# A hybrid trunk on one core: the samples' new SSD state is written to the increment's tile and stored from there; low parts of fresh y blocks read the transposed block in PSUM

## The chip, the cores and the metric

One core of one Trainium2 chip runs the whole program, both layers, in one launch. The metric is the device time of an execution in microseconds (us). The kernel before was run three times; one further execution was profiled, and all rows below are of that one.

## What is computed

A trunk of two layers works on a prompt of 2048 tokens and on 8 samples of one token each, with the same weights. Cut to what matters here:

```python
def _layer(x, ...):
    u = _rmsnorm(x, norm_w) @ w_in                 # 1024 -> 4880, columns split among the groups
    ...
    ya = mLSTM group  (512 wide), times its gates
    yb = SSD group    (512 wide), times its gate, normed
    yc = sliding-window attention with sinks (512 wide), times its gate
    y = concat([ya, yb, yc]) @ w_out               # 1536 -> 1024
    return x + y, states

def _ssd step:  h_t = exp(dt_t A) h_{t-1} + dt_t x_t B_t^T ;  y_t = h_t C_t
```

The outputs are y of the prompt and of the samples and every state array after the step; for the samples that includes the new SSD state h of each layer and sample (8 heads x 64 x 128 values).

## The kernel before, in words

**Blocks and chunks.** The prompt goes through in blocks of 512 tokens, four to a layer, eight in all; below, "the first out phase" is the out projection of block 0 of layer 0, and so on to the eighth. Every large product is a sum of three fp32r products of high and low parts. The weights come in chunks of 128 rows: `load_chunk` brings a chunk, `split_chunk` makes its high part on ScalarE (line 494) and low part on GpSimd (line 498) the first time, and `multiply` does 12 matmuls of 128x512 into four PSUM banks (`pj`; line 519 where the weights stream, line 521 where they stand still). An out phase has 24 chunks, two halves of the output by the 12 blocks k of y (k = 0 to 3 mLSTM, 4 to 7 SSD, 8 to 11 attention). For all but the last block of the trunk, the out phase of a block comes after the first five column groups (g0, qk, v, o, z) of the next block; after it come x0, x1, cq, cz, bz.

**Side streams.** The mixing of a block (mLSTM `a`, SSD `b`, attention `c`), the convolution `v`, gates, norms and the samples' work `d` are Python generators. `pump` takes a step of one of them between matmuls when a planner's model of the engines (`Clock`: its costs for each engine, and when the next of the four other PSUM banks, `mx`, is free) says so; `drain` forces a stream to its end at a few chunks: `b` at the last chunk of v, `a` at that of o, `a` and `d` at that of cq, and `c` ahead of the first chunk of an out phase. A scheduler then orders every engine's instructions. So a change of one instruction's operands can move others.

**prep_y (line 1243).** Ahead of each out chunk it makes the high and the low part of a y block. The first time a block k < 8 is used (half 0: 64 such fresh blocks in the program), it lies token-major: TensorE transposes it into an `mx` bank `pt` (4 x line 1252), ScalarE writes the high part `yh` from the bank (line 1259), and ScalarE copies the bank back into the block (line 1263). For every block VectorE then makes the low part `yl` = block x norm weight - `yh` from SBUF (line 1266, `low`, put off by half a chunk). The chunk's matmuls need `yh` first and `yl` for the third product of each tile.

**dec_b (line 1477).** The SSD step of the 8 samples, in the second out phase of each layer. Each sample b has three tiles of a set, `h`, `t`, `bb`, and the two sets take turns. The steps are: SyncE loads the old state of sample b+1 into `h` (line 1547) and its broadcast B and C into `bb` (line 1548, from `bcd`); GpSimd `h` = h x exp(dt A) (1560); VectorE `t` = B x (dt x) (1562); GpSimd `h` = h + t (1564); SyncE stores `h` (1566); VectorE `t` = h x C (1567) and reduces `t` to y (1568). The load of sample b+2 into the same `h` therefore waits for the store of sample b to land.

**dec_c (line 1588)** is the samples' attention in the first out phase of each layer: scores are multiplied on GpSimd (1659), reduced on VectorE into `dST` (1661), and transposed on TensorE for the softmax (1667, 1668).

Of the kernel before, what the change touches and what calls it, by code (L numbers as in the profile page):

```python
# [16 lines left out]
ALU = mybir.AluOpType  # L17
AX = mybir.AxisListType
# [166 lines left out]
class Build:  # L185
# [1057 lines left out]
    def prep_y(self, ch):  # L1243

        nc, S, k = self.nc, ch['S'], ch['k']
        Y, L = [S['yA'], S['yB'], S['yC']][k // 4], S['L']
        blk = Y[:, :, (k % 4) * 128:(k % 4) * 128 + 128] if k < 8 else Y[:, k % 4, 0:512].rearrange("p (t c) -> p t c", c=128)
        new = ch['new']
        if new:
            pt = self.mx()  # L1250
            for t in range(4):
                nc.tensor.transpose(pt[:, t * 128:t * 128 + 128], blk[:, t, :], self.ident)  # L1252
            pt = pt.rearrange("p (t c) -> p t c", c=128)
        else:
            pt = blk
        i = k % 2

        yh, yl = (self.xTh[i], self.xTl[i]) if S['last'] else self.F[2 * i:2 * i + 2]
        nc.scalar.activation(yh.rearrange("p (t c) -> p t c", c=128), pt, AF.Copy, scale=L['ynw'][:, k:k + 1])  # L1259

        if new:

            nc.scalar.activation(blk, pt, AF.Copy)  # L1263

        def low():
            nc.vector.scalar_tensor_tensor(yl.rearrange("p (t c) -> p t c", c=128), blk, L['ynw'][:, k:k + 1],  # L1266
                                           yh.bitcast(F32).rearrange("p (t c) -> p t c", c=128),
                                           op0=ALU.mult, op1=ALU.subtract)

        self.late.append((0, low))  # L1270
        ch['y'] = (yh, yl)
# [205 lines left out]
    def dec_b(self, l, L, D):  # L1477
        nc, I, O, U = self.nc, self.I, self.O, self.U[5:]
        TT = nc.vector.tensor_tensor
# [18 lines left out]
        for half in range(2):  # L1498
# [9 lines left out]
            acc, t = xc[:, half * 4:half * 4 + 4, :], self.s([128, 4, 8], "dct")  # L1508
# [30 lines left out]
        yT = self.s([128, 8, 4], "dyT")  # L1539
        yield  # L1540

        def sets(b):
            return [U[(1 + 3 * (b % 2) + i) % 6][:, 0:512] for i in range(3)]

        def load(b):
            h, t, bb = sets(b)
            nc.sync.dma_start(h.rearrange("p (j s) -> p j s", s=128), I['state_ssm'][l, b].rearrange("(j h) p s -> (h p) j s", h=2))
            nc.sync.dma_start(bb, bcd[b].partition_broadcast(128))
# [3 lines left out]
        for b in range(8):  # L1552
            if b < 7:
                load(b + 1)
            h, t, bb = sets(b)
            h3, t3 = [x.rearrange("p (j s) -> p j s", s=128) for x in (h, t)]
            Bv, Cv = [bb[:, i * 256:i * 256 + 256].rearrange("p (g s) -> p g s", s=128).unsqueeze(2).to_broadcast([128, 2, 2, 128])
                      for i in range(2)]
            t4, h4 = [x.rearrange("p (g j s) -> p g j s", g=2, s=128) for x in (t, h)]
            nc.gpsimd.tensor_tensor(h3, h3, dAp[:, b, :].unsqueeze(2).to_broadcast([128, 4, 128]), op=ALU.mult)  # L1560
            xb = dtp[:, b, :].unsqueeze(2).to_broadcast([128, 4, 128]).rearrange("p (g j) s -> p g j s", g=2)
            TT(t4, Bv, xb, op=ALU.mult)
            yield
            nc.gpsimd.tensor_tensor(h, h, t, op=ALU.add)
            yield
            nc.sync.dma_start(O['s_h'][l, b].rearrange("(j h) p s -> (h p) j s", h=2), h3)
            TT(t4, h4, Cv, op=ALU.mult)
            nc.vector.tensor_reduce(yT[:, b, :], t3, AX.X, ALU.add)
            yield
        xD = self.s([128, 8, 4], "dxD")  # L1570
        TT(xD, xT.rearrange("p j b -> p b j"), Dp.unsqueeze(1).to_broadcast([128, 8, 4]), op=ALU.mult)
# [5 lines left out]
        t = U[0][:8, 0:512]  # L1577
# [358 lines left out]
```

## Time and profile before

| | us |
|---|---|
| three runs: median (lowest to highest) | 2995.44 (2991.24 to 2997.36) |
| the profiled execution: its own time | 2994.12 |
| its span in the profile | 2992.3 |
| TensorE busy within the span | 2903.5 (97%) |
| VectorE, ScalarE, GpSimd busy | 1912.3, 1235.0, 920.3 |

The span is what the profile covers; 1.8 us of the execution lie outside it. A row of a timeline gives start, duration, engine, line, operation and tiles, and in brackets the idle time of the engine just before it with what ended that. A row of a table of stretches gives the busy time of each engine within the stretch.

### The profile page before, as it was taken

To read this page: it belongs to the slowest core of one execution; us is meant where nothing else is said; L and a number is where in the kernel's file an instruction comes from. 1 tells how busy PE (TensorE), PEld (TensorE's weight loads), DVE (VectorE), ACT (ScalarE), POOL (GpSimd) and SP (SyncE) were. 2 spreads that over 40 slices of the span, in tenths; PEclk is the share of its full clock that TensorE was granted. 3 is DMA by queue.
4 is the path that set the end of the run, shared out by engine and by line. 5 is a ranking of instruction groups with operands and counts; after the bars stand their busy time and mean duration, and the time that the engine had idled before them with its cause. 6 is when DMAs were issued, how large, how long until landed. Compare 5 with 4: busy or idle time off the path is not lost.

```text
span 2992.3 us, 42253 instructions
## 1 busy us (share of the span) xinstructions
PE 2903.5 (97%) x14454; PEld 2373.4 (79%) x14454; DVE 1912.3 (64%) x4323; ACT 1235.0 (41%) x3219; POOL 920.3 (31%) x968
## 2 busy tenths in 40 slices
PE   8999999999999999999999999999999999999988
PEld 7787877788878888888788778887887778788876
DVE  6378567778476763477644686477755677645774
ACT  5343555235432453325544345432444225532344
POOL 5336325244131430116422552332421132200321
PEclk9999999999999999999999999999999999999999
DMA  8755558754575434655556745687545754355533
GB/s 279 241 197 168 174 184 284 248 170 141 164 247 189 151 117 143 199 171 182 184 187 215 240 159 183 205 274 232 161 156 177 244 174 160 131 163 165 177 112 124
DMA packets 245995, 558.82 MB, mean 187 GB/s; under 512 B 49308, under 2 KB 82236, under 8 KB 245732
## 3 DMA queue, kind: packets, MB, share of 16 engines
q1 hardware_dynamic: 245780, 556.12, 57.6%
q8 instruction: 114, 1.87, 0.3%
q14 instruction: 101, 0.83, 0.1%
HBM read 430.46 MB, written 127.87 MB: 187 GB/s over the span
## 4 chain that ended last, share of the span: by engine, by line
PE 71%; DVE 13%; DMA 8%; POOL 3%; ACT 2%; issue 2%; SPq 1%; POOLq 0%; DVEq 0%; ACTq 0%
PE pj L519 29%; PE pj L521 27%; DMA wr<-in_w_in 2%; PE mx L1203 2%; PE mx L1152 2%; PE mx L984 1%; DMA unit<-bcd 1%; DVE quad L659 1%; PE mx L542 1%; PE mx L541 1%; POOL hl L498 1%; ACT unit L1173 1%; PE mx L993 1%; PE mx L1252 1%; DMA unit<-us 1%
## 5 line engine op out<-in xcount | busy, mean ns | idle before, releaser
L521 PE MATMUL pj<-hl,xTh 128*128 128x512 f32 (+1 forms) x3072 | 945.4, 383 | 17.2 <-ACT hl L494 7.6
L519 PE MATMUL pj<-xTh,hl 128*128 128x512 f32 x2240 | 727.5, 402 | 4.8 <-ACT xTh L1259 2.9
L521 PEld LDWEIGHTS pj<-hl,xTh 128*128 128x128 f32 x3072 | 564.6, 189 | 129.0 <-DVE quad L562 8.3
L521 PE MATMUL pj<-hl,xTl 128*128 128x512 f32 (+1 forms) x1536 | 580.4, 381 | 0.0
L519 PE MATMUL pj<-parts,hl 128*128 128x512 f32 x2016 | 518.9, 404 | 15.1 <-DVE parts L1266 8.3
L519 PEld LDWEIGHTS pj<-xTh,hl 128*128 128x128 f32 x2240 | 421.5, 190 | 100.9 <-ACT xTh L1259 3.9
L519 PEld LDWEIGHTS pj<-parts,hl 128*128 128x128 f32 x2016 | 366.9, 189 | 96.1 <-DVE parts L1266 11.2
L519 PE MATMUL pj<-xTl,hl 128*128 128x512 f32 x1120 | 436.0, 398 | 1.9 <-DVE xTl L1266 1.9
L498 POOL TENSOR_TENSOR hl<-wr,hl 128x512 fp32r<-128x512 f32 (+1 forms) x232 | 318.9, 1380 | 356.3 <-ACT hl L494 311.2
L521 PEld LDWEIGHTS pj<-hl,xTl 128*128 128x128 f32 x1536 | 291.1, 189 | 52.5
L1195 POOL TENSOR_TENSOR parts<-parts,cst 128x512 fp32r<-128x512 f32 x120 | 158.6, 1339 | 409.0 <-ACT parts L1188 392.3
L519 PEld LDWEIGHTS pj<-xTl,hl 128*128 128x128 f32 x1120 | 211.2, 189 | 47.7 <-DVE xTl L1266 2.3
L1266 DVE SCALAR_TENSOR_TENSOR parts<-quad,lp,parts 128x512 fp32r<-128x512 f32 x168 | 143.0, 852 | 155.4 <-ACT quad L1263 62.4
L494 ACT ACTIVATE hl<-wr 128x512 fp32r<-128x512 f32 (+1 forms) x232 | 142.2, 615 | 234.2 <-PE mx L542 49.6
L1032 POOL TENSOR_TENSOR unit<-quad,rpqn 128x256 f32<-128x256 f32 x32 | 24.3, 759 | 441.6 <-PE mx L951 166.8
L1173 ACT ACTIVATE unit<-unit,c_m,c_sc 128x128 f32<-128x128 f32 x256 | 123.3, 483 | 69.3 <-DVE c_m L1164 68.8
L1259 ACT ACTIVATE parts<-quad,lp 128x512 fp32r<-128x512 f32 x112 | 80.4, 720 | 155.9 <-PE pj L519 141.1
L659 DVE SCALAR_TENSOR_TENSOR quad<-quad,lp,quad 128x512 f32<-128x512 f32 x192 | 141.8, 781 | 0.3
L1189 DVE TENSOR_TENSOR parts<-mx,parts 128x512 fp32r<-128x512 f32 x64 | 44.0, 687 | 90.2 <-ACT parts L1188 81.0
L384 POOL TENSOR_TENSOR quad<-quad 128x512 f32<-128x512 f32 x24 | 33.5, 1398 | 217.1 <-ACT quad L382 216.4
L1181 ACT ACTIVATE unit<-unit,c_m 128x128 f32<-128x128 f32 x256 | 81.3, 392 | 19.4 <-DVE c_m L1179 19.2
L541 PE MATMUL mx<-hl,samS 128*66 128x512 f32 (+1 forms) x208 | 83.4, 403 | 0.9 <-ACT hl L494 0.9
(409 smaller groups left out, 4551.3 us busy)
## 6 DMA issues: line engine op xcount, KB each, us to landing
hl<-kept SPq DMA_DIRECT2D x552, 512.0 KB
kept<-hl SPq DMA_DIRECT2D x184, 512.0 KB
wr<-in_w_in SPq DMA_DIRECT2D x168, 256.0 KB
hl<-kept SPq DMA_DIRECT2D x48, 272.0 KB
quad<-in_xT SPq DMA_DIRECT2D x40, 256.0 KB
quad<-in_x_prompt SPq DMA_DIRECT2D x16, 512.0 KB
wr<-in_w_out SPq DMA_DIRECT2D x32, 256.0 KB
x<-quad SPq DMA_DIRECT2D x32, 256.0 KB
```

The costliest lines, as they stand in the source:

```text
L494: nc.scalar.activation(h, r, AF.Copy)
L498: nc.gpsimd.tensor_tensor(lw, r, h.bitcast(F32), op=ALU.subtract)
L519: nc.tensor.matmul(ps[t], w[:, tt], a, start=st and first, stop=en and last)
L521: nc.tensor.matmul(ps[t][:, :N], a[:, tt], w[:, :N], start=st and first, stop=en and last)
L541: nc.tensor.matmul(pd[:66, :N], self.samS[:, k, :], hi[:, :N], start=st, stop=False)
L659: nc.vector.scalar_tensor_tensor(acc, u[:, j:j + 512], cw[:, j, c:c + 1], acc, op0=ALU.mult, op1=ALU.add)
L1152: nc.tensor.matmul(o, q, kz[:, a, s, 0:nk, :].rearrange("p n c -> p (n c)"), start=s == 0, stop=s == 1)
L1173: nc.scalar.activation(P(a, j), P(a, j), AF.Exp, bias=nm[:, j:j + 1], scale=head(sc, a, j), accum_out=den[:, j:j + 1])
L1181: nc.scalar.activation(P(a, j), P(a, j), AF.Copy, scale=den[:, j:j + 1])
L1195: nc.gpsimd.tensor_tensor(o.bitcast(F32R), p, self.triu.unsqueeze(1).to_broadcast([128, 4, 128]), op=ALU.mult)
L1259: nc.scalar.activation(yh.rearrange("p (t c) -> p t c", c=128), pt, AF.Copy, scale=L['ynw'][:, k:k + 1])
L1266: nc.vector.scalar_tensor_tensor(yl.rearrange("p (t c) -> p t c", c=128), blk, L['ynw'][:, k:k + 1], yh.bitcast(F32).rearrange("p (t c) -> ...
```

## The change

```diff
@@ prep_y
         def low():
-            nc.vector.scalar_tensor_tensor(yl.rearrange("p (t c) -> p t c", c=128), blk, L['ynw'][:, k:k + 1],
+            nc.vector.scalar_tensor_tensor(yl.rearrange("p (t c) -> p t c", c=128), pt, L['ynw'][:, k:k + 1],
                                            yh.bitcast(F32).rearrange("p (t c) -> p t c", c=128),
                                            op0=ALU.mult, op1=ALU.subtract)
@@ dec_b
-            nc.gpsimd.tensor_tensor(h, h, t, op=ALU.add)
-            yield
-            nc.sync.dma_start(O['s_h'][l, b].rearrange("(j h) p s -> (h p) j s", h=2), h3)
-            TT(t4, h4, Cv, op=ALU.mult)
-            nc.vector.tensor_reduce(yT[:, b, :], t3, AX.X, ALU.add)
+
+            nc.gpsimd.tensor_tensor(t, h, t, op=ALU.add)
+            yield
+            nc.sync.dma_start(O['s_h'][l, b].rearrange("(j h) p s -> (h p) j s", h=2), t3)
+            TT(h4, t4, Cv, op=ALU.mult)
+            nc.vector.tensor_reduce(yT[:, b, :], h3, AX.X, ALU.add)
             yield
```

In `prep_y` the low part of the 64 fresh blocks takes its first operand from the PSUM bank `pt` in place of the block in SBUF (for other blocks `pt` is the block, and nothing changes). In `dec_b` the new state is written over `t`, stored from `t`, and the product with C goes to `h`. From line 1564 on, a line of the changed kernel has a number one higher.

No engine gets an instruction more or less. The order of the instructions moves in two long stretches, from the start of each layer's first out phase to the end of its second (438 to 891 us of the profile, and 1917 to 2367 us; the tables of the profile cut them into eight, four to a layer: the first out phase, the chunks x0 to bz, g0 to z, the second out phase); elsewhere a few rows move. Three places:

**TensorE, start of the sixth out phase (layer 1, block 1).** `mx_21084` and `mx_21130` are the banks of the transposed y blocks k = 0 and 1, `hl_20995` the last chunk of bz, `hl_21032` the first out chunk, `mx_21000` and `mx_21051` banks of the attention's mixing. Before:

```order
L521 MATMUL pj_20938<-hl_20981,xTh_110 128x512
L1252 MATMUL mx_21084<-ident,quad_100 128x128
L1203 MATMUL mx_21051<-parts_94,vd 128x512
L1252 MATMUL mx_21084<-ident,quad_100 128x128 x3
L521 MATMUL pj_20935<-hl_20995,xTh_111 128x512
```

With the change:

```order
L1203 MATMUL mx_21000<-parts_93,vd 128x512
L521 MATMUL pj_20938<-hl_20995,xTh_111 128x512
L1203 MATMUL mx_21000<-parts_94,vd 128x512
L1203 MATMUL mx_21051<-parts_91,vs 128x512
L1252 MATMUL mx_21084<-ident,quad_100 128x128 x4
L1203 MATMUL mx_21051<-parts_92,vs 128x512
L1252 MATMUL mx_21130<-ident,quad_100 128x128 x4
L1203 MATMUL mx_21051<-parts_93,vd 128x512
L519 MATMUL pj_21124<-parts,hl_21032 128x512 x2
```

The transposes of k = 0 stood ahead of all 12 matmuls of the last bz chunk; now they stand behind it, and behind them only the four of k = 1 and two of the mixing come ahead of the out phase's first matmul.

**TensorE, the softmax transposes of dec_c, layer 0.** `hl_5452` is the last chunk of x1, `hl_5481` the first of cq, `hl_5635` the last of cq. Before:

```order
L519 MATMUL pj_5365<-xTh_111,hl_5452 128x512
L1667 MATMUL mx_5687<-ident,dST_5258 64x128
L1668 MATMUL mx_5687<-ident,unit_84 64x128
L521 MATMUL pj_5568<-hl_5481,xTh_104 128x512
```

With the change (the same two, one line number higher):

```order
L521 MATMUL pj_5561<-hl_5612,xTh_110 128x512
L1668 MATMUL mx_5712<-ident,dST_5378 64x128
L1669 MATMUL mx_5712<-ident,unit_84 64x128
L521 MATMUL pj_5558<-hl_5635,xTh_111 128x512
```

They moved from ahead of the first cq chunk to ahead of the last one, seven chunks or 84 matmuls later; in layer 1 they moved alike.

**VectorE, dec_b of layer 1 around samples 2 and 3.** `unit_85` to `unit_87` are h, t, bb of the even samples, `unit_88`, `unit_89`, `unit_84` those of the odd ones. Before:

```order
L792 TENSOR_TENSOR rtA_21443<-mx_21439,cst 120x512
L1562 TENSOR_TENSOR unit_86<-unit_87,ddt_21333 128x512
L1562 TENSOR_TENSOR unit_89<-unit_84,ddt_21333 128x512
L838 TENSOR_TENSOR unit_83<-mx_21446,X_20560 128x256
L1266 SCALAR_TENSOR_TENSOR parts_92<-quad_97,lp_2958,parts_91 128x512
L1567 TENSOR_TENSOR unit_86<-unit_85,unit_87 128x512
```

With the change:

```order
L1568 TENSOR_TENSOR unit_88<-unit_89,unit_84 128x512
L1266 SCALAR_TENSOR_TENSOR parts_92<-quad_97,lp_2958,parts_91 128x512
L838 TENSOR_TENSOR unit_83<-mx_21446,X_20560 128x256
L1569 TENSOR_REDUCE dyT_21342<-unit_88 128x4
L1562 TENSOR_TENSOR unit_86<-unit_87,ddt_21333 128x512
L1266 SCALAR_TENSOR_TENSOR parts<-quad_97,lp_2958,parts 128x512
L1562 TENSOR_TENSOR unit_89<-unit_84,ddt_21333 128x512
```

The rows at line 1562 are those of samples 2 and 3 in both. They stood back to back, ahead of two low parts (line 1266); now one low part stands ahead of both, and one between them.

## Rows read from the trace of the kernel before

**Rows 1.** The page: busy time of each engine (section 1).

```profile
PE 2903.5 (97%) x14454; PEld 2373.4 (79%) x14454; DVE 1912.3 (64%) x4323; ACT 1235.0 (41%) x3219; POOL 920.3 (31%) x968
```

**Rows 2.** Stretches: second out phase of each layer, and the sum over all eight.

```profile
core 0: us, PE busy (x) PEld busy (x) DVE busy (x) ACT busy (x) POOL busy (x), PEclk, DMA share, GB/s
...
797.10:890.70 93.60, 87.48 (x449) 70.36 (x447) 71.17 (x135) 34.49 (x87) 25.71 (x18) 1.00 0.70 221
...
2271.00:2366.80 95.80, 87.16 (x445) 70.16 (x443) 65.58 (x132) 32.06 (x83) 19.34 (x15) 1.00 0.69 215
sum 902.50, PE 875.74 PEld 718.89 DVE 626.86 ACT 373.81 POOL 282.98; mean PE 109.47 PEld 89.86 DVE 78.36 ACT 46.73 POOL 35.37
```

**Rows 3.** What TensorE waited for, whole span: us, times, longest.

```profile
PE pj L519 <- DVE parts L1266: 8.3, 8, 2.4
...
PE mx L1667 <- DVE dST L1661: 4.2, 2, 3.6
```

**Rows 4.** Timeline, fresh block k=5, second out phase of layer 0.

```profile
816.18 0.75 DVE L1266 SCALAR_TENSOR_TENSOR parts<-quad,lp,parts 128x512 fp32r<-128x512 f32 x1 [0.95 <-ACT quad L1263]
...
820.97 1.29 PE L519 MATMUL pj<-parts,hl 128*128 128x512 f32 x4
```

**Rows 5.** Timeline, the fresh block whose low part ended with least to spare.

```profile
1170.88 0.75 DVE L1266 SCALAR_TENSOR_TENSOR parts<-quad,lp,parts 128x512 fp32r<-128x512 f32 x1 [3.90 <-ACT quad L1263]
...
1172.98 3.04 PE L519 MATMUL pj<-parts,hl 128*128 128x512 f32 x12
```

**Rows 6.** Line 1266: what ended VectorE's idle time before it, us, times.

```profile
  ACT quad L1263: 68.0, 37
```

**Rows 7.** VectorE by line and shape: busy us, mean ns.

```profile
L1266 DVE SCALAR_TENSOR_TENSOR parts<-quad,lp,parts 128x512 fp32r<-128x512 f32 x168 | 143.0, 852 | 155.4 <-ACT quad L1263 62.4 <-PE pj L519 54.2 <-ACT parts L1259 36.8
...
L562 DVE SCALAR_TENSOR_TENSOR quad<-wP,pj 128x512 f32<-128x512 f32 x64 | 41.4, 680 | 5.5 <-ACT wP L561 5.2
```

**Rows 8.** Timeline, fresh block k=1, first out phase of layer 0.

```profile
440.73 0.61 ACT L1263 ACTIVATE quad<-mx 128x512 f32<-128x512 f32 x1
...
444.22 1.04 PE L1252 MATMUL mx<-ident,quad 128*128 128x128 f32 x8
...
445.07 0.75 DVE L1266 SCALAR_TENSOR_TENSOR parts<-quad,lp,parts 128x512 fp32r<-128x512 f32 x1
```

**Rows 9.** Timeline, softmax transposes of the samples' attention, layer 0.

```profile
580.49 0.69 DVE L1661 TENSOR_REDUCE dST<-unit 128x8 f32<-128x512 f32 x1 [2.54 <-POOL unit L1659]
...
581.23 0.30 PE L1667 MATMUL mx<-ident,dST 128*64 128x128 f32 x1 [3.65 <-DVE dST L1661]
```

**Rows 10.** VectorE's waits in the SSD update, layer 0, then layer 1.

```profile
DVE unit L1562 <- DMA unit<-bcd: 5.9, 4, 3.4
...
DVE unit L1562 <- DMA unit<-bcd: 11.6, 6, 3.2
```

**Rows 11.** SyncE queue's waits, the same two stretches.

```profile
SPq L1547 <- DMA out_s_h<-unit: 7.2, 5, 3.5
...
SPq L1547 <- DMA out_s_h<-unit: 6.5, 4, 3.3
```

**Rows 12.** Timeline, SSD update of layer 1, samples 0 to 3.

```profile
2299.84 0.69 DVE L1568 TENSOR_REDUCE dyT<-unit 128x4 f32<-128x512 f32 x1
...
2301.81 0.32 SPq L1548 DMA_DIRECT2D unit<-bcd  x1
2302.18 0.43 SPq L1547 DMA_DIRECT2D unit<-in_state_ssm  x1
...
2307.84 0.69 DVE L1562 TENSOR_TENSOR unit<-unit,ddt 128x512 f32<-128x512 f32 x1 [2.81 <-DMA unit<-bcd]
...
2311.83 1.51 DVE L1567 TENSOR_TENSOR unit<-unit,unit 128x512 f32<-128x512 f32 x1 [2.30 <-POOL unit L1564]
...
2313.26 1.75 DVE L1266 SCALAR_TENSOR_TENSOR parts<-quad,lp,parts 128x512 fp32r<-128x512 f32 x1
...
2315.06 1.20 PE L519 MATMUL pj<-parts,hl 128*128 128x512 f32 x4 [2.43 <-DVE parts L1266]
```


## The prediction

> **What bounds the kernel now.** I read the page first, then a table of stretches, then the list of what TensorE waited for, and timelines only where that list or the order of the instructions pointed. On the page TensorE is busy for 2903.5 us [rows 1], 97% of the span of 2992.3, so all its idle time is about 89 us. The order moves in eight stretches only, and there the granted clock is 1.00 throughout, the full 2.4 GHz; the sum row gives 902.5 us of width and 875.7 of TensorE [rows 2]. So 26.8 us of idle time is all that the moved order could give back, and a loss has to come as new idle time. Of the idle time, 6.1 us (93.6 - 87.5) lie in the second out phase of layer 0 and 8.6 (95.8 - 87.2) in that of layer 1 [rows 2]. The list of waits says what ends such time: low parts of y, 8.3 us in 8 waits, and the reduction `dST` of the samples' attention, 4.2 us in 2 [rows 3]. A measurement of this kernel tells about 0.2%, 6 us, from no change, so the whole case lies close to that size.
>
> **The low part from PSUM.** What the text of the change suggests is that `low` need not wait for ScalarE's copy back. The trace has that wait: VectorE stood idle 68.0 us in 37 waits until line 1263 had ended [rows 6]. That is VectorE's time and not TensorE's. In the second out phase the low part of block k=5 runs from 816.18 to 816.93. Its chunk begins with eight matmuls that read the high part alone, and the four that read the low part start at 820.97 [rows 4]. In the tightest of the 56 fresh blocks outside the last out phase the low part starts at 1170.88, ends 0.75 later at 1171.63, and its first reader starts at 1172.98 [rows 5]: 1.35 us to spare. So an earlier low part is worth nothing to TensorE; what hides it is the eight of twelve matmuls that need the high part alone and come first.
>
> Nor will it be much earlier. The built program still makes each of the 64 fresh low parts wait on the second ScalarE instruction, the copy, since both read one bank. A shorter one it may be: line 562, the same operation with one operand in PSUM, takes 680 ns, against 852 ns mean here [rows 7], some 0.75 undisturbed; 64 x 0.07 = 4.5 us to 64 x 0.17 = 11 us of VectorE, spread over the whole program, and off TensorE's path by the spare time above. I set the term at 0.
>
> **The bank is held longer.** Before, a bank of transposed y was free when the copy ended; now it is free when the low part has ended. In most blocks the low part follows the copy at once, so this is some 0.7 us, in a ring of four banks whose next use is planned with more room than that. Where VectorE is late it is more: for k=1 of the first out phase the copy ended at 441.34, the low part ran from 445.07 to 445.82, and TensorE's transposes into a bank of that ring started at 444.22 [rows 8]. If that bank was the next in line, they would now start 1.6 us later (445.82 - 444.22). I find four such places in the eight out phases, of the size 0.5 to 1.9 us. Below, the cost is 0 (the matmul that then comes late is followed by others that do not wait, and a scheduler that sees the hold reorders); above, 4 x 1.6 = 6.4. I take 1, near the lower end, since the row shows VectorE behind there through other work and the transposes some 2.6 us ahead of the chunk they feed.
>
> The Trainium skill has a rule that speaks against this half (the page "PSUM — Partial Sum Buffer", section "PSUM bank collisions raise a hardware error"): two different engines must not access the same bank in the same 32 partitions at once, two reads included. By it the low part cannot run beside the copy, as the program's wait on the copy has it, and the hold is 0.7 us; without it the low part could run beside the copy and the hold would be about 0.2. The sum would be the same within 1 us, and no run so far has a low part that reads PSUM.
>
> **The order around the samples' attention.** In layer 0 `dST` is reduced from 580.49 to 581.18, and TensorE stands 3.65 us before its transposes at 581.23 [rows 9]. The list gives 4.2 for the two layers [rows 3]. With the change these transposes stand 84 matmuls later in both layers, some 20 us at the pace of the row in which 12 take 3.04 us [rows 5]. The wait goes: **-4.2**. Bounds: 0, if the whole stream behind it shifts as far, and -4.2. I take the whole since only steps of the samples' stream feed `dST`, and those lag by 10 to 36 matmuls against 84.
>
> **dec_b.** The load of sample b+2's state now waits for the reduction of sample b, its last reader, and not for a store to land. SyncE's queue waited 7.2 and 6.5 us for stores to land [rows 11]. In layer 1 the reduction of sample 0 ended at 2300.53 (2299.84 + 0.69) and the load was issued at 2302.18 [rows 12]: it can go 1.65 us earlier. What depended on it: VectorE at 2311.83 had stood 2.30 us for GpSimd's addition, the low part behind it ran from 2313.26 to 2315.01, and TensorE at 2315.06 had stood 2.43 for that [rows 12]. So up to 1.65 of this one wait goes. The other wait, for B and C, stays: the broadcast is issued at 2301.81 and ends VectorE's wait at 2307.84 [rows 12], and its load needs the product with C as before. There VectorE waited 5.9 us in layer 0 and 11.6 in layer 1 [rows 10]; by the new order, with low parts ahead of and between the two multiplications that wait, I estimate that three samples of a layer still wait (sample 3 for 2.7, near the 2.81 of its row, samples 4 and 7 for 1 each), 4.7 in each layer, so 1.2 + 6.9 = 8.1 of VectorE's waiting goes. A new wait comes: the multiplication into `t` (line 1562) for b+2 must await the landing of the store of b from `t`. That store goes out two steps before, the longest wait for its landing was 3.5 us [rows 11], and the multiplication stands behind the load of B and C in any case; I set it at 0, with the 7.2 and 6.5 that SyncE's queue had as the upper bound. TensorE feels VectorE only through the low parts, 8.3 us of waits in all [rows 3]. Between 0 and 8.3 I take half: **-4**.
>
> **Starts of out phases.** In the sixth out phase the transposes of k=0 lost a lead of 12 matmuls, 3.0 us by the same pace. A fresh block needs its transposes and the high part ahead of its first matmul. From the end of the copy back through two ScalarE instructions of 0.6 to 0.7 us [rows 8] that is an estimate of 1.2 us with the hops between engines, partly behind the four transposes of k=1 and the mixing that stand between. About 1.0 there; the same bunching is milder in the second out phase (k=0 from 12 to 3 matmuls) and for k=6 in both, 0.5 each time taken together: **+2**. Bounds 0 and 4 x 1.2 = 4.8. The mixing of the blocks lags by 9 to 14 us behind the samples' steps through the quiet stretches and catches up at the drains; TensorE had next to no idle time there and does the same work, so **+1** for a wait at a drain.
>
> **The sum.** Against the profiled execution of 2994.1: -4.2 - 4 + 1 + 2 + 1 = -4.2, so 2989.9. That execution lies 1.3 below the median of the runs, 2995.4, and within them; the same sum from the median gives 2991.2. I say **2991**.
>
> **Rivals.**
> - *Both waits go.* TensorE's waits for low parts vanish and not half of them: -4.2 - 8.3 + 4 = -8.5, from the median 2987. For it: the load of the state is the late one in the row at 2302.18, and the reduction that now releases it is early. Against it: the broadcast's wait of 2.81 at 2307.84 stays [rows 12]. It decides where VectorE's wait for GpSimd's addition falls to zero in both layers.
> - *It does not do what it says.* The low part still starts after the copy, the load of the state is not the last to arrive, and the reduction of `dST` shifts with its transposes; costs are hidden too: 2995, as the median.
> - *Slower: the bank becomes the bound.* Transposes and mixing share four banks, and each fresh block holds one for 0.7 us more, up to 4.5 where VectorE is late [rows 8]. If in half of the 64 fresh blocks half of the hold falls on TensorE, 32 x 0.35 = 11.2; with -4.2 and +2 that is +9, so 3004. It decides from about 12 us of new waiting before transposes and mixing matmuls; below that it is eaten up by the gains. For it: the slips of 0.5 to 1.9 us in four places. Against: in most places the low part follows the copy at once, as in [rows 4], and the planner knows the hold.
>
> **How the numbers follow.** The forecast gets 0.45, from 2988 to 2995; of that 0.10 lies below 2989.4, 0.2% under the median. Both waits going gets 0.26, all but wholly faster than that; the change that does nothing 0.15, within 0.2%; the slower case 0.14. So faster 0.36, same 0.35 + 0.15 = 0.50, slower 0.14. The range runs from 2983, the rival's 2987 less the 4 that the costs of starts and banks may not take, to 3001, the forecast plus the upper bounds of banks and starts (5.4 and 2.8) and some of the runs' own spread; most of the slower case is left out.
>
> **What would show it.** TensorE's waits for `dST` should be gone. Waits of SyncE's line 1547 for stores should be gone too, and VectorE's at line 1562 for the broadcast should stand near 5 in each layer. VectorE should still wait for the copy before most fresh low parts, which should take about 0.69 us. TensorE's idle time in the second out phases should fall from 6.1 and 8.6 to some 4 and 7. I would be wrong if line 1252 or 1203 showed new waits for a bank by several us, if line 1562 waited for a store, or if idle time came up at the drains that the samples' steps had moved into.

## The result, and the profile after

The changed kernel takes 3010.02 us (median of 4 runs, 3008.33 to 3013.05) against 2994.41 (4 runs, 2991.24 to 2997.36): 1.0053 of the time before, 95% interval 1.0037 to 1.0069, so 11 to 21 us slower. The forecast was 2991, the range ended at 3001, and slower had 0.14.

The page of the changed kernel, its span and the busy times [rows 1]:

```profile
span 3006.6 us, 42241 instructions
PE 2913.3 (97%) x14454; PEld 2378.9 (79%) x14454; DVE 1915.5 (64%) x4323; ACT 1234.8 (41%) x3219; POOL 923.4 (31%) x968
```

TensorE is busy 9.8 us longer (2913.3 - 2903.5) with the same 14454 instructions. The table of stretches, cut at the same matmuls of the program as for the kernel before (header as in [rows 2]; the stretches are, in order: g0, qk and v; o and z; the second out phase, all of layer 0; then layer 1 from the middle of x0 to the end of cq, and its second out phase; the sum is over all ten):

```profile
658.00:744.20 86.20, 82.95 (x476) 70.98 (x474) 62.88 (x145) 49.18 (x145) 33.77 (x33) 1.00 0.46 153
744.20:804.50 60.30, 57.61 (x269) 46.84 (x268) 30.25 (x98) 30.84 (x90) 11.45 (x9) 0.97 0.50 159
804.50:902.40 97.90, 90.11 (x449) 72.64 (x448) 72.14 (x135) 34.92 (x88) 24.13 (x18) 0.97 0.67 211
...
2026.70:2093.30 66.60, 60.55 (x256) 48.51 (x255) 44.46 (x95) 14.42 (x42) 12.68 (x8) 0.95 0.70 226
...
2284.70:2380.80 96.10, 90.50 (x453) 72.21 (x452) 68.70 (x135) 34.42 (x87) 21.69 (x17) 0.98 0.67 216
sum 919.00, PE 887.97 PEld 726.07 DVE 628.48 ACT 371.50 POOL 288.76; mean PE 88.80 PEld 72.61 DVE 62.85 ACT 37.15 POOL 28.88
```

The three of these that have no row in [rows 2], in the kernel before, and the same sum:

```profile
660.70:743.90 83.20, 83.20 (x484) 72.01 (x483) 67.27 (x163) 50.63 (x147) 33.70 (x32) 1.00 0.48 153
743.90:797.10 53.20, 53.20 (x252) 43.46 (x251) 20.32 (x69) 26.94 (x81) 10.15 (x8) 1.00 0.53 167
...
2017.40:2077.50 60.10, 58.24 (x253) 45.96 (x253) 44.39 (x96) 15.81 (x44) 10.90 (x8) 1.00 0.76 253
...
sum 902.50, PE 875.74 PEld 718.89 DVE 626.86 ACT 373.81 POOL 282.98; mean PE 87.57 PEld 71.89 DVE 62.69 ACT 37.38 POOL 28.30
```

So g0 to v take 86.2 us for 83.2, o and z 60.3 for 53.2, the second out phase 97.9 for 93.6 [rows 2], and in layer 1 the stretch to the end of cq takes 66.6 for 60.1. The other six are between 1.2 longer (x0 to bz of layer 0) and 2.2 shorter. In all it is 919.0 - 902.5 = 16.5 us, against 14.3 of the spans. Of these 16.5, TensorE's busy time has 888.0 - 875.7 = 12.2, for 4443 rows of matmuls and transposes where there were 4445, and idle time only 4.3 (31.0 for 26.8). That 4.3 is a balance: the four stretches that got longer by 3 us and more have 11.8 us more idle time between them, the other six 7.5 less. The column of the granted clock bears on the busy time: 0.95 to 0.98 in four stretches that stood at 1.00. **In this pair of profiles most of the loss is matmuls at a lower clock.** A profile is one execution; the end of the experiments takes all of them together, and there the clock has about half.

One place shows how. Windows of 4 us of the changed kernel, where cq begins in layer 1:

```profile
2060.00:2064.00 4.00, 3.68 (x16) 2.64 (x14) 4.00 (x6) 2.02 (x4) 2.18 (x2) 1.00 0.82 271
2064.00:2068.00 4.00, 0.00 (x0) 0.00 (x0) 3.93 (x5) 1.17 (x5) 1.52 (x2) 0.82 0.65 195
2068.00:2072.00 4.00, 3.29 (x8) 2.62 (x9) 2.35 (x4) 2.54 (x9) 1.06 (x1) 0.50 0.89 196
2072.00:2076.00 4.00, 4.00 (x16) 3.23 (x15) 2.34 (x4) 0.00 (x0) 1.27 (x1) 0.82 0.33 134
2076.00:2080.00 4.00, 4.00 (x18) 3.22 (x18) 4.00 (x8) 0.63 (x1) 0.00 (x0) 1.00 0.40 134
```

TensorE does nothing for 4 us and more, then the granted clock is 0.50, half speed (1.2 for 2.4 GHz), while it works again; in the next window it is 0.82, and from 2076 on 1.00. What it waited for, whole span (us, times, longest):

```profile
PE pj L519 <- DVE parts L1266: 8.6, 6, 3.8
PE pj L521 <- ACT quad L622: 7.4, 2, 5.0
...
PE mx L1152 <- DVE parts L1120: 2.7, 2, 2.1
```

The waits for `dST` [rows 3] are gone, as forecast. In their place stands line 622, ScalarE's evacuation of x1's PSUM banks into the convolution, 7.4 us in two waits, one in each layer; cq's matmuls need those banks. It is not in the list of before at all. The waits for low parts are fewer (6 for 8) and longer (3.8 for 2.4).

Why line 622 is late is read from VectorE's rows ahead of it in layer 1 (after):

```profile
2042.34 0.69 DVE L1662 TENSOR_REDUCE dST<-unit 128x8 f32<-128x512 f32 x1 [5.18 <-POOL unit L1660]
...
2043.04 4.33 DVE L821 SCALAR_TENSOR_TENSOR quad<-quad,ml,quad 128x128 f32<-128x128 f32 x12
2047.29 0.53 DVE L657 TENSOR_SCALAR quad<-quad,lp 128x512 f32<-128x512 f32 x1
...
2063.78 2.95 DVE L651 SCALAR_TENSOR_TENSOR quad<-quad,quad 128x512 f32<-128x512 f32 x3
...
2067.26 0.68 DVE L651 SCALAR_TENSOR_TENSOR quad<-quad,quad 128x512 f32<-128x512 f32 x1
2067.97 0.20 ACT L621 ACTIVATE quad<-hist 128x3 f32<-128x3 f32 x1 [0.99 <-DVE quad L651]
2068.08 1.07 ACT L622 ACTIVATE quad<-pj 128x512 f32<-128x512 f32 x2
2068.71 0.79 PE L521 MATMUL pj<-hl,xTh 128*128 128x512 f32 x1 [5.02 <-ACT quad L622]
```

and from those of the kernel before at the same work:

```profile
2027.83 0.69 DVE L1661 TENSOR_REDUCE dST<-unit 128x8 f32<-128x512 f32 x1 [12.02 <-POOL unit L1659]
...
2029.69 0.54 DVE L657 TENSOR_SCALAR quad<-quad,lp 128x512 f32<-128x512 f32 x1
...
2049.63 0.68 DVE L651 SCALAR_TENSOR_TENSOR quad<-quad,quad 128x512 f32<-128x512 f32 x1
...
2053.96 0.69 DVE L1661 TENSOR_REDUCE dST<-unit 128x8 f32<-128x512 f32 x1 [1.93 <-POOL unit L1659]
```

Line 621, ahead of line 622 on ScalarE, waits for the last pieces of the convolution (line 651). Before, VectorE stood for GpSimd's product early (2027.83, 12.02 us) and had the last of these pieces done at 2050.31, ahead of the end of x1; the last reduction, which TensorE did wait for a little [rows 3], comes at 2053.96. After, the first reduction into `dST` (line 1662) stands 5.18 us for GpSimd ahead of the convolution, the mixing's line 821 follows, and the last piece ends at 2067.94, when TensorE has stood since 2063.7.

Counted from the start of the stretch (2017.4 before, 2026.7 after), the first reduction starts at 15.6 us for 10.4, the convolution's line 657 behind it at 20.6 for 12.3, and the last piece ends at 41.2 for 32.9. So all of the 8.3 us of delay is there when the convolution begins: 5.2 with the late step of the samples' attention, 3.1 between it and line 657, where line 821 now stands.

### The profile page after: what moved, and what is told of

Its sections match the earlier page's. It is cut to its first block, busy times and chain, and to the rows that moved or that the text cites. A ratio compares the mean times of both kernels' runs of the same rounds, so it can differ in the third digit from the quotient of the medians.

```text
span 3006.6 us, 42241 instructions
## 1 busy us (share of the span) xinstructions
PE 2913.3 (97%) x14454; PEld 2378.9 (79%) x14454; DVE 1915.5 (64%) x4323; ACT 1234.8 (41%) x3219; POOL 923.4 (31%) x968
## 4 chain that ended last, share of the span: by engine, by line
PE 75%; DVE 12%; DMA 6%; POOL 2%; issue 2%; ACT 2%; SPq 0%; POOLq 0%; DVEq 0%; ACTq 0%
PE pj L519 32%; PE pj L521 28%; PE mx L1203 2%; PE mx L1152 2%; PE mx L984 1%; PE mx L542 1%; PE mx L541 1%; DVE quad L443 1%; DMA unit<-bcd 1%; DMA hl<-kept 1%; PE mx L1252 1%; DMA quad<-x 1%; PE mx L850 1%; PE mx L857 1%; PE mx L1186 1%
## 5 line engine op out<-in xcount | busy, mean ns | idle before, releaser
L521 PEld LDWEIGHTS pj<-hl,xTh 128*128 128x128 f32 x3072 | 565.4, 190 | 136.8 <-DVE quad L562 8.6
L519 PEld LDWEIGHTS pj<-xTh,hl 128*128 128x128 f32 x2240 | 421.8, 190 | 103.7 <-ACT xTh L1259 3.9
L519 PEld LDWEIGHTS pj<-parts,hl 128*128 128x128 f32 x2016 | 369.6, 190 | 95.4 <-DVE parts L1266 11.6
L1266 DVE SCALAR_TENSOR_TENSOR parts<-quad,lp,parts 128x512 fp32r<-128x512 f32 x112 | 100.6, 903 | 93.4 <-PE pj L519 61.2
L653 ACT ACTIVATE quad<-quad 128x512 f32<-128x512 f32 x64 | 40.5, 634 | 137.8 <-DVE quad L659 137.3
L815 ACT ACTIVATE unit<-quad 128x128 f32<-128x128 f32 x128 | 39.7, 310 | 135.6 <-DVE quad L873 133.2
```

The lines of the kernel that those rows point to most:

```text
L519: nc.tensor.matmul(ps[t], w[:, tt], a, start=st and first, stop=en and last)
L521: nc.tensor.matmul(ps[t][:, :N], a[:, tt], w[:, :N], start=st and first, stop=en and last)
```

## Experiments

The two halves of the change, and the two things that the first half does, were taken apart. To separate the moved order from the chip's own hold on the bank, some kernels tell the planner another operand than the instruction has. The edit common to them (shortened, shown with the low part from SBUF and the planner told PSUM):

```diff
 Clock.run
-        for i in code[self.n:]:
+        for at, i in enumerate(code[self.n:], self.n):
+            seen = self.as_if.get(at, {})
...
                 m = self.key(x)
+                m = seen.get(m, m)
 prep_y, low
+            self.clock.run()
             nc.vector.scalar_tensor_tensor(yl..., blk, L['ynw'][:, k:k + 1], ...)
+            if new:
+                self.clock.as_if[self.clock.n] = {key of blk: key of pt}
```

Times below are medians and, in brackets, the ratio to the kernel before on the same chip with its 95% interval; 0.001 is 3.0 us. The ratio is estimated from all executions, so it is not exactly that of the two medians.

**order_only**: the edit above on the kernel before.

> The kernel before, in which the low part still reads the block in SBUF, but the planner's model is told that it reads the PSUM bank; dec_b as before. So it has the moved order without the hold on the bank. If the moved order is the cause (theory ORDER): +9 to +15 us on the kernel before, with TensorE's new waits for line 622 at the start of cq and a granted clock under 1.00 around them. If the hold on the bank is the cause (theory BANK): within 3 us of the kernel before. If dec_b's new tiles are (theory DEC_B): within 3 us of the kernel before.

3009.65 us for 2997.52 (1.0038, 1.0026 to 1.0051). No instruction reads anything else than before, and 8 to 15 us are lost: ORDER. The wait for the evacuation of x1 (line 626 there) is 8.7 us.

**psum_old_order**: `pt` in the low part, and the planner told `blk`.

> The low part reads the PSUM bank, but the planner's model is told that it reads the block in SBUF, so that the order stays nearly that of the kernel before; dec_b as before. The hold on the bank without the moved order. ORDER: within 3 us of the kernel before, the wait for dST still there. BANK: +9 to +15 us, with new waits of TensorE's lines 1252 and 1203. DEC_B: within 3 us of the kernel before.

3000.45 for 2997.52 (1.0010, 1.0002 to 1.0019). The hold on the bank, together with the little that the order still differs, costs 0.6 to 5.7 us. BANK falls as the main cause, though the hold is not free.

**low_part_alone**: the first hunk of the change only.

> Only the change in prep_y, dec_b as before. ORDER: +10 to +15 us, the waits for line 622 and for line 1120 and the lowered clock as with the whole change; what is missing to +15 is dec_b's share. BANK: +9 to +15 us as well. DEC_B: within 3 us of the kernel before.

3012.62 for 2997.52 (1.0056, 1.0044 to 1.0068). The two pieces add up: 12.1 + 2.9 = 15.0 against 15.1 by the medians. Each of the three is known to 3 or 4 us either way, so that the sum comes out so close is luck.

**dec_b_alone**: the second hunk only.

> Only the change in dec_b, prep_y as before. ORDER and BANK: -4 to +3 us, in the second out phases alone. DEC_B: +5 to +15 us, with a wait for low parts of some 4 us and a lowered clock in both second out phases.

2997.84 for 2997.52 (1.0003, 0.9994 to 1.0012). DEC_B falls; the gain I had forecast for it does too.

Where does the order come off? The planner runs while the program is built, so what it decides can be written down. Its record of the first steps that differ, in the first out phase of layer 0. The number behind P counts the calls of `pump`; "since" and the numbers behind "ahead" say whether the stream's last step is done and how far the engines run ahead; the number behind the name of the bank is how long that bank, the next one of the ring, has been free. All are the planner's own count in ns, no times of the chip. Told `blk`:

```
P 449 d credit 2.35 pe 459673 since 459423 ahead {'DVE': 1249, 'Act': 565, 'Poo': -215} back 3300.0 mx mx_714_4357 451 GO
```

Told `pt`:

```
P 449 d credit 2.35 pe 459673 since 459423 ahead {'DVE': 1249, 'Act': 565, 'Poo': -215} back 3300.0 mx mx_714_4357 -1499 no
P 450 d credit 2.5 pe 460328 since 460078 ahead {'DVE': 594, 'Act': -90, 'Poo': -870} back 3300.0 mx mx_714_4357 -844 no
P 451 d credit 2.5 pe 460983 since 460733 ahead {'DVE': -61, 'Act': -745, 'Poo': -1525} back 3300.0 mx mx_714_4357 -189 no
P 452 d credit 2.5 pe 462274 since 462024 ahead {'DVE': -1352, 'Act': 573, 'Poo': -2815} back 3300.0 mx mx_715_4370 2563 GO
```

The bank is that of y block k=4. By the planner's count its low part now holds it for 1.95 us more (451 + 1499), and `pump` refuses the same step of the samples' stream three times. It asks for a free bank ahead of every stream's steps, whether the step takes a bank or not. From there on the record of that stream differs: 19 of its 180 steps come by a drain, where 12 did. Two kernels test whether this one block is enough. **one_refused** is order_only with `if new and S['b'] == 0 and k == 4`, and **one_allowed** is the whole change with the planner told `blk` under that condition.

> The kernel before, with the planner's model told that the low part reads the PSUM bank for one y block alone: k=4 of block 0, once in each layer, 2 of the 64 fresh blocks. All reads and dec_b stay as before. Theory CASCADE (the planner refuses one step of the samples' stream at that block since it counts the bank as taken, and everything that follows of that stream is late and gets drained): as much as with all 64, +9 to +13 us, the wait for line 622 at the start of cq in layer 1 among it. Theory SUM (many small delays at many blocks add up): under +3 us.

3016.57 for 2995.98 (1.0061, 1.0045 to 1.0077): some 18 us lost (13 to 23) by what the planner believes of 2 of 64 reads. CASCADE, and over the +9 to +13 that I expected. That it is more than with all 64 is not shown: the interval reaches into those of order_only and of the whole change. Line 626, the evacuation of x1 there, has 9.3 us of TensorE's waits. Its stretches (g0 to v; o and z; then layer 1 to the end of cq) are those of the changed kernel:

```profile
661.10:747.00 85.90, 82.99 (x475) 71.02 (x475) 62.86 (x145) 49.10 (x145) 33.85 (x33) 1.00 0.47 152
747.00:806.80 59.80, 57.61 (x270) 46.77 (x269) 30.34 (x98) 30.83 (x90) 11.44 (x9) 0.97 0.53 162
...
2030.10:2097.60 67.50, 60.80 (x256) 48.54 (x255) 44.53 (x95) 14.34 (x42) 12.88 (x8) 0.95 0.67 220
```

> The whole change (low parts from PSUM in all 64 blocks, dec_b's tiles), with the planner's model told the old operand for k=4 of block 0 alone, 2 of the 64. CASCADE: -8 to -13 us against the changed kernel, so 0 to +5 us on the kernel before. SUM: +12 to +15 us on the kernel before, as the changed kernel.

2997.37 for 2995.98 (1.0008, 0.9996 to 1.0021). With the other 62 told the truth, and all 64 reading PSUM, nearly the whole loss is gone.

**full_old_order**: the whole change, the planner told `blk` for all 64.

> The whole change, with the planner told the old operand for all 64 blocks. If the two parts add up: +3 us of the low part from PSUM without the moved order, and 0 of dec_b, so +1 to +5 us on the kernel before. If dec_b's new tiles gain only where the bank is held longer, below 0; if they hurt there, over +6.

3000.63 for 2995.98 (1.0010, 1.0000 to 1.0020): as expected if the two parts add up, 0.1% for the bank and nothing for dec_b, though no loss at all is just within the interval.

**samples_not_gated**, and the same once more:

```diff
 pump
-                if st[4] <= now and max(ck.t.values()) <= now + back and ck.free_at(self.rings['mx'][-4]) <= now:
+                if st[4] <= now and max(ck.t.values()) <= now + back and (st[3] == 'd' or ck.free_at(self.rings['mx'][-4]) <= now):
```

> The whole change, and pump no longer asks for a free bank ahead of steps of the samples' stream d (most of which take none). CASCADE: the samples' steps keep their place, no wait for line 622 over 3 us in layer 1, and 0 to +5 us on the kernel before. SUM: +10 us or more, since the other streams still see the held banks.

2993.54 for 2995.98 (0.9989, 0.9979 to 0.9999). CASCADE: line 622 is not in the list of TensorE's waits, and the wait for `dST` is back (4.4 us). The time lies even below the 0 to +5 us that I gave it.

> The same kernel as the run samples_not_gated (the whole change without the question for a free bank ahead of the samples' steps), once more, since its interval of 0.9979 to 0.9999 only just leaves out no difference. If the gain is its own (theory GAIN): the interval again ends below 1.0000, the median 2 to 4 us under the kernel before. If it was the spread of the runs (theory SPREAD): an interval that holds 1.0000.

2996.15 for 2995.30 (0.9998, 0.9986 to 1.0010): SPREAD. The whole change with one question less in `pump` is as fast as the kernel before, and no faster. **low_part_not_gated** is the same with dec_b as before, and **d_v_s_not_gated** the whole change with the question waived for the streams d, v and s.

> The change in prep_y alone, with pump no longer asking for a free bank ahead of the samples' steps. If dec_b's tiles gain 0 also in this order: within 2 us of the whole change without the gate (2993.5 against 2996.0 of the kernel before). If they gain where TensorE waits for low parts: +2 to +6 us on that, mostly in the second out phase of layer 1, which lost 5.6 us there.

2995.82 for 2996.49 (1.0003, 0.9994 to 1.0012): dec_b's tiles are worth nothing in this order either, within some 4 us.

> The whole change, with the question for a free bank waived for the samples' steps, the convolution's and the norm sums'. Few of these were refused for it, so within 2 us of the version that waives it for the samples alone: -5 to 0 us on the kernel before.

2995.42 for 2996.49 (1.0005, 0.9996 to 1.0015). Nothing more to get there. No version of this study beats the kernel before.

**samples_held**: the whole change, with the samples' stream held back for two more column groups, so that `dST` stands behind the convolution on VectorE (edit shortened).

```diff
 pump
-            if st[1] >= 1.0 and self.open(st):
+            if st[1] >= 1.0 and self.open(st) and not (st[3] == 'd' and self.now_g in ('x0', 'x1')):
 multiply
+        self.now_g = ch['g']
```

> The whole change, but pump takes no step of the samples' stream d while the chunks of x0 and x1 run; its rest is drained at the last cq chunk. In this order VectorE's reductions into dST of layer 1 stand behind the convolution and not ahead of it. Theory HEAD (a reduction that waits for GpSimd stands ahead of the convolution on VectorE, so the evacuation of x1 is late and TensorE stands at the first cq chunk): TensorE's waits for line 622 fall from 7.4 to under 2 us and the 6.5 us that layer 1 lost up to there do not come; what they were comes back at most by half at the drain of cq, so 2 to 6 us under the changed kernel. Theory LOAD (VectorE has too much to do between the out phase and cq, in whatever order): the wait for line 622 stays over 4 us, and the time is that of the changed kernel or more.

3032.46 for 2996.49 (1.0132, 1.0115 to 1.0149): 34 to 45 us lost, where the changed kernel loses 11 to 21. At its place HEAD held: the evacuation (line 624 there) is not in the list of TensorE's waits at all, and the stretch to the end of cq takes 57.2 us, less than before. The rest of the expectation was wrong by far: the bill comes later. Stretches of this kernel (layer 0: x0 to bz, g0 to v; layer 1: the second half of x0 to cq, then cz and bz, then g0 to z) and its waits for GpSimd and `dST`:

```profile
527.70:651.80 124.10, 122.57 (x564) 98.91 (x563) 78.80 (x209) 30.11 (x70) 32.99 (x44) 1.00 0.66 214
651.80:755.50 103.70, 94.01 (x517) 79.36 (x515) 72.87 (x167) 53.86 (x153) 46.92 (x51) 0.95 0.38 124
...
2040.40:2097.60 57.20, 57.20 (x253) 46.34 (x252) 41.22 (x111) 14.53 (x39) 5.80 (x9) 1.00 0.70 225
2097.60:2156.00 58.40, 54.01 (x239) 42.44 (x238) 32.54 (x87) 10.77 (x22) 23.16 (x33) 0.94 0.49 160
2156.00:2309.90 153.90, 144.75 (x767) 122.84 (x766) 95.57 (x252) 73.60 (x214) 43.05 (x50) 0.97 0.47 149
```

```profile
PE mx L995 <- POOL unit L991: 8.8, 3, 3.8
...
PE mx L1670 <- DVE dST L1664: 5.6, 2, 4.1
```

Layer 0 gains 8.6 us up to bz (124.1 for 132.7), where 47 fewer matmuls and transposes run (564 for 611), and loses 20.5 from g0 to v (103.7 for 83.2); layer 1 loses 17.1 from g0 to z (153.9 for 136.8), with the clock at 0.95 and 0.97. In these two stretches 33 and 32 more matmuls and transposes run (517 for 484, 767 for 735), and TensorE now stands for GpSimd (line 995, 3.8 us in each). My reading is that the mixing of the block waits behind the late samples' steps and has to catch up before the drains at v and o, so that a late stream is paid for in the streams behind it. No run tests that.

**All executions together.** The record has the span and the mean granted clock of every execution, and span times clock is what it would have taken at full clock throughout. Mean span and mean clock, for the kernel before on the same chip and then for the run: order_only 2995.3 us at 0.9891, then 3005.9 at 0.9878; low_part_alone the same, then 3011.1 at 0.9862; one_refused 2994.5 at 0.9893, then 3014.1 at 0.9867. By that estimate 4, 9 and 8 us of the 11, 16 and 20 lost go with the lower clock, and 6, 7 and 11 would be lost without it. It gives the clock rather too much, since a low clock while TensorE stands idle costs nothing. So the clock has about half of the loss. The table of stretches shows more, since the kernel before, at 0.991 in its profile, has none of its low clock there; its executions in the experiments have 0.989 on average, and go from 2987 to 3004 us.

## Why the prediction was wrong

- **The step that failed is the last term of "Starts of out phases".** It saw that the mixing "lags by 9 to 14 us behind the samples' steps through the quiet stretches and catches up at the drains", and priced that at +1, since TensorE "had next to no idle time there and does the same work". order_only measures what the order costs, 8 to 15 us, with the gain at `dST` and the loss at the starts of out phases in it, which came to -1.2 with this term (-4.2 + 2 + 1). Little idle time is no cover: it says that the stretch has no slack, and the steps that are late come due in it. From g0 to z of layer 0 idle time went from 0 to 5.9 us, and from the middle of x0 to the end of cq in layer 1 from 1.9 to 6.1. The term had no upper bound either, so nothing of it is in the range. The last of my signs of being wrong, idle time at the drains that the samples' steps had moved into, is near what happened: the longest wait stands at the start of cq, seven chunks ahead of their drain.
- **The bound under it was wrong too**: "a loss has to come as new idle time". In the two profiles only 4.3 of the 16.5 us were idle time; 12.2 were the same matmuls, slower. Over all executions about half of the loss goes with the lower clock. In the place shown the clock fell behind a long pause. That the matmuls behind a stall can be slower I had not put into any case.
- **dST, -4.2**: the wait did go. But I looked at the transposes alone, and did not ask what the late reductions would hold up on VectorE. In layer 1 it is the convolution, and behind it line 622, 7.4 us in both layers: more than the wait that went.
- **dec_b, -4**: measured 0 (-1.8 to 3.6 us). SyncE's line 1547 waits for no store to land any more, line 1562 waits for none either, and VectorE's waits for B and C went from 11.6 to 7.9 us in layer 1 [rows 10], 5.9 as before in layer 0, where I had 4.7 for both. Waits of VectorE in the second out phase of the changed kernel, layer 0 then layer 1, and of SyncE's queue in layer 1:

```profile
DVE unit L1562 <- DMA unit<-bcd: 5.9, 4, 2.8
...
DVE unit L1562 <- DMA unit<-bcd: 7.9, 5, 3.1
```

```profile
SPq L1547 <- DVE dyT L1569: 1.3, 2, 0.9
```

  But a low part still stands behind such a wait. In layer 0 of the changed kernel:

```profile
848.00 0.83 DVE L1562 TENSOR_TENSOR unit<-unit,ddt 128x512 f32<-128x512 f32 x1 [2.77 <-DMA unit<-bcd]
...
848.75 1.74 DVE L845 TENSOR_TENSOR unit<-unit,lim 128x512 f32<-128x512 f32 x1
...
850.42 1.52 DVE L1266 SCALAR_TENSOR_TENSOR parts<-quad,lp,parts 128x512 fp32r<-128x512 f32 x1
...
852.00 1.22 PE L519 MATMUL pj<-parts,hl 128*128 128x512 f32 x2 [3.73 <-DVE parts L1266]
```

  VectorE waits 2.77 us for B and C, does line 845 in 1.74 us and the low part in 1.52, and TensorE has stood for 3.73; the granted clock of that second out phase is 0.97. The half of the low parts' waits that I had taken off did not go: they total 8.6 us for 8.3. TensorE's idle time in the second out phases is 7.8 and 5.6 us, where I had some 4 and 7.
- **The low part from PSUM, 0**: right that it starts no earlier. It still waits for the copy (71.6 us in 42 waits, 68.0 in 37 before [rows 6]), as the rule of the Trainium skill on PSUM banks says it must (the page "PSUM — Partial Sum Buffer", section "PSUM bank collisions raise a hardware error"); no run here lets the two reads overlap, so what would follow wasn't seen. Wrong that it is shorter: 751 ns for 752, but for the few beside GpSimd (last section).

```profile
L1266 DVE SCALAR_TENSOR_TENSOR parts<-quad,lp,parts x112: 732/752/1887, 466.5 to 2713.7; 128x512 fp32r<-128x512 f32 x112
L1266 DVE SCALAR_TENSOR_TENSOR parts<-mx,lp,parts x56: 731/751/753, 437.1 to 2658.0; 128x512 fp32r<-128x512 f32 x56
...
  ACT quad L1263: 71.6, 42
```

- **The bank, +1**: 0.6 to 5.7 us by psum_old_order. Its size is within the bounds I gave (0 to 6.4), but not its place: no transpose of line 1252 waits for a bank in the list of the changed kernel. In the one profile of psum_old_order the difference lies in layer 0's second out phase (99.6 us for 93.6, clock 0.97), where VectorE's order differs a little; that this is the whole of it was not shown.
- **The rival that came true in sign** had the bank as the bound on the chip. Slower came out for another reason than the one it gives. It named the right resource in the wrong place: the bank was short in the planner's books, at one block, and the planner then moved everything behind it.

What stays open: how much of the loss would remain if the clock did not fall. The 6 to 11 us above are an estimate, and no run holds the order and takes the pauses away. Nor is it settled why of two pauses one is followed by half speed and another is not: the kernel before stood 3.65 us for `dST` [rows 9] at a clock of 1.00 throughout, and dec_b_alone in its profile stood 2.63 us for the same transposes and had 0.57 in the window behind it. The windows behind these pauses, before and then dec_b_alone:

```profile
584.00:588.00 4.00, 4.00 (x19) 3.22 (x18) 4.00 (x15) 0.00 (x0) 0.00 (x0) 1.00 0.02 6
...
584.00:588.00 4.00, 4.00 (x13) 3.14 (x12) 3.79 (x17) 0.00 (x0) 0.00 (x0) 0.57 0.30 121
```

## What to carry to other kernels

Where a planner or a scheduler sets the order, a change of one operand is first of all a change of what the planner believes. So look for its first decision that differs, ask which stream that makes late, and price the lateness at every deadline behind it, not only at the waits that the profile of before shows. To tell the order's cost from the instruction's, build both mixed kernels: the old instruction with the new belief, and the new one with the old. And on an engine that is 97% busy look at the granted clock behind every new pause: here the slower matmuls had about half of the loss. One profile of each kernel was not enough to size that share.

## What the runs showed of the hardware

VectorE's 128x512 low part took 751 ns (median) with one operand in PSUM and 752 with all in SBUF, where line 562, of the same operation, takes 680 [rows 7]. But the longest of the 56 from PSUM took 753 ns, and the longest of the 112 from SBUF 1887. The long ones lie where GpSimd has its tensor operations, most in the two first out phases (the samples' attention), others beside the samples' SSD step, as at 850.42 (1.52 us).

The fresh blocks allow a comparison at one place, since they are read from SBUF before and from PSUM after. For k=3 of the first out phase, before and then after, with GpSimd's line 498 beside it:

```profile
450.77 1.29 POOL L498 TENSOR_TENSOR hl<-wr,hl 128x512 fp32r<-128x512 f32 x1 [9.14 <-ACT hl L494]
...
451.74 0.88 DVE L1266 SCALAR_TENSOR_TENSOR parts<-quad,lp,parts 128x512 fp32r<-128x512 f32 x1 [0.84 <-ACT quad L1263]
...
448.50 1.30 POOL L498 TENSOR_TENSOR hl<-wr,hl 128x512 fp32r<-128x512 f32 x1 [8.93 <-ACT hl L494]
...
449.47 0.75 DVE L1266 SCALAR_TENSOR_TENSOR parts<-mx,lp,parts 128x512 fp32r<-128x512 f32 x1 [0.83 <-ACT quad L1263]
```

This one took 870 to 880 ns in the four profiles that read SBUF and 750 or 751 in the ten that read PSUM. Over all 14 profiles, without the last out phase, 88 low parts from PSUM had a GpSimd operation beside them for over 30% of their time, and none took more than 753 ns; of the 26 fresh ones from SBUF with as much beside them, 21 took 815 to 1770. So it is both: beside GpSimd the low part got longer in most cases with all operands in SBUF, and in none with one in PSUM. Alone, the operand made no difference. In this kernel it buys nothing (psum_old_order is no faster than the kernel before); few fresh blocks have GpSimd beside them.
